# Weight loads issued in turn by SyncE and by GpSimd

## The chip, the cores and the metric

The kernel runs on one core of a Trainium2 chip. The metric is the device time of one execution in microseconds. The kernel before took 2195.15 us as the median of three runs (2191.74, 2195.15 and 2196.63 us).

## The reference, cut to what matters

The program is a decoder trunk of two layers on 256 tokens of width 2048, all in float32:

```python
# layer 0
proj  = h @ even_w_in                       # 2048 -> 4096: pool | q | k | v
mixed = concat(pool_mixer(p), stick_breaking_attention(q, k, v))
h = layer_norm(a * h + mixed @ even_w_out)
h = layer_norm(a * h + (silu(h @ w_gate) * (h @ w_up)) @ w_down)      # 5632 wide
# layer 1
z = gelu(h @ odd_w_in); u, v = split(z)
h = layer_norm(a * h + (u * (W_s @ layer_norm(v) + b)) @ odd_w_out)
for e in range(8):                          # every expert, 1408 wide, top 2 of 8 per token
    y += gates[:, e] * swiglu(h, w_gu[e], w_down[e])
h = layer_norm(a * h + y)
```

Some 520 MB of weights are read once each, and nearly all work is the products with them.

## The kernel before, in words

A weight matrix is cut into pieces of 128 rows by up to 4 x 512 columns (1 MB; some of 768 KB in the experts, and small ones at the start). The helper `load` (line 99) handles one piece: it takes a buffer `raw` (a pool of 5, line 894), starts the DMA into it (line 108), lets ScalarE round it to the high part `wh` (line 109), and subtracts to get the low part `wl` (line 117). `wh` and `wl` have 4 buffers each (line 895). The subtraction is VectorE's; a few, named by `plan` around the layer norms, and the second half of the last, shorter piece of each expert's down projection (`tail`) are GpSimd's. `raw` becomes free when the subtraction has read it, and the DMA that next takes that buffer waits for that.

For every slice of 128 rows TensorE runs three products (`mm3`, lines 126 to 128): x high by `wh`, x high by `wl`, x low by `wh`. A 1 MB piece is 12 matmuls of 512 columns for each tile of 128 tokens. In the dense stages each piece serves two token tiles, so 24 matmuls. In the experts the tokens of an expert are gathered by a matmul with a selection matrix into one tile of 128, so a piece serves 12 matmuls only. Expert by expert there are 24 pieces for gate and up and 12 for down (four blocks of three: 1 MB, 1 MB, 768 KB), 288 pieces in all, after 231 pieces before them.

The stages follow each other in one stream: the input projection with attention and pooling beside it, the output projection, the feed-forward part, the gating layer with its two projections, the routing, eight experts, the final norm. The order of instructions on each engine is made by a list scheduler when the program is built, from its own estimates; an engine works through its list in order and waits at the head of it. All DMAs are SyncE's: weight pieces, the inputs at the start (`xraw`, line 287), the norms' rows (`gb`, line 179), and the output (line 746). GpSimd's list holds 38 subtractions, some work of the routing and of the final norm, and nothing else.

At the end of the program stands a branch for experts with more than 128 tokens; it is not entered with these inputs.

Of the kernel before, what the change touches and what calls it, by code (L numbers as in the profile page):

```python
# [74 lines left out]
class Trunk:  # L75
# [23 lines left out]
    def load(self, src, w=CB, tail=None):  # L99

        nc = self.nc
        fence, planned = self.plan.pop(0) if self.plan else (None, nc.vector)
        src = src.rearrange("p (k n) -> p k n", n=w)
        kc = src.shape[1]
        raw = self.praw.tile([P, kc, w], F32, tag="raw", name="raw")
        wh = self.pw.tile([P, kc, w], F32R, tag="wh", name="wh")
        wl = self.pw.tile([P, kc, w], F32R, tag="wl", name="wl")
        nc.sync.dma_start(raw, src)
        nc.scalar.copy(wh, raw)  # L109
        if tail is not None:  # L110
            cuts = [(0, tail, nc.vector), (tail, kc, nc.gpsimd)]
        elif planned is nc.gpsimd:
            cuts = [(k, min(k + HALF, kc), planned) for k in range(0, kc, HALF)]
        else:
            cuts = [(0, kc, planned)]
        for a, b, eng in cuts:
            self.after(eng.tensor_tensor(wl[:, a:b, :], raw[:, a:b, :], wh[:, a:b, :].bitcast(F32), ALU.subtract),  # L117
                       fence)
        return wh, wl, kc
# [768 lines left out]
    def build(self):  # L888
        nc, ctx, i = self.nc, self.ctx, self.i
        e = ctx.enter_context  # L890
        pc = e(self.pool("const"))
        self.psm = e(self.pool("small"))
        self.pln = e(self.pool("ln", 2))
        self.praw = e(self.pool("raw", 5))
        self.pw = e(self.pool("w", 4))
        self.punit = e(self.pool("units", 17))
        self.pacc = e(self.pool("acc", 4, space=bass.MemoryType.PSUM))
        self.pps = e(self.pool("ps", 4, space=bass.MemoryType.PSUM))
        self.c = pc.tile([P, C_MAIN], F32, tag="c", name="c")
        self.plan = []  # L900
        self.fill = []
        self.lncols = pc.tile([P, 4, KC], F32, tag="lncols", name="lncols")
        self.ident = self.c[:, C_IDENT:C_IDENT + P]
        self.iota1 = self.c[:, C_IOTA1:C_IOTA1 + P]
        nc.scalar.preload_act_table_set("natural_log_exp_and_others")
        zeros = self.unit("zeros", BF16, [P, CB])
        nc.vector.memset(zeros, 0.0)
        self.keep_busy(10, zeros)

        mlhs = self.even_mixer()  # L910
        ph = e(self.pool("h", side="right"))
        self.h = [ph.tile([P, D], F32, tag=f"h{t}", name=f"h{t}") for t in range(NT)]
        for t in range(NT):
            nc.sync.dma_start(self.h[t], i["x"][t * P:(t + 1) * P, :])
        xT, yT = {}, {}
        _, G, B = self.out_proj(i["even_w_out"], mlhs, i["even_ln1_g"], i["even_ln1_b"],
                                norm=lambda t, stats: self.ln_to_lhs(t, stats, 0, xT))
        G, B = self.ffn(xT, G, B, lambda t, stats: self.ln_to_lhs(t, stats, 1, yT))
        mlhs = self.sgu(yT, G, B)
        pm = e(self.pool("moe", side="right"))  # L920
        self.pm = pm
        self.router_prep(pm)
        stats, G, B = self.out_proj(i["odd_w_out"], mlhs, i["odd_ln1_g"], i["odd_ln1_b"], self.router_step)
        self.moe(pm, stats, G, B)
# [81 lines left out]
```

## Time and profile before

| what | value |
|---|---|
| median of 3 runs | 2195.15 us |
| the profiled execution's own time | 2192.12 us |
| its span, first to last instruction | 2190.4 us |
| TensorE busy | 2147.6 us (98%) |
| VectorE, ScalarE, GpSimd busy | 1469.1, 1143.4, 96.4 us |
| moved by DMA | 537.81 MB, all weights on one queue |
| granted TensorE clock, mean | 0.991 |

Rows of groups give line, engine, operation, tiles and count, then busy time and the mean of one in ns, then how long the engine was idle before them and who ended that. Rows of waits give who waited for whom, the total in us, how often, and the longest. The busy time of matmuls is the union of overlapping records, so the pace of TensorE is read as stretch divided by count.

### The profile page before, as it was taken

Reading aid. Unit: us, or ns where it says so; the run is one execution under the profiler, and the core shown is the slowest. Engines: PE = TensorE matmul, PEld = TensorE weight load, DVE = VectorE, ACT = ScalarE, POOL = GpSimd, SP = SyncE. Lnnn points to the kernel's source line nnn. Section 1 sums busy time; section 2 is a strip of 40 time slices with the busy share of each in tenths; the row PEclk is TensorE's granted clock in tenths of the full one; section 3 lists DMA queues with packets and bytes.
Section 4 is the critical chain, followed back from the end, with each engine's and each line's share of the span. In section 5 each row is a group of like instructions: output and inputs, shape, how many; then the busy total and the mean of one; then the engine's idle time right before and its main releaser. Section 6 shows DMA issues by size and latency. Waiting matters only on the chain.

```text
span 2190.4 us, 24556 instructions
## 1 busy us (share of the span) xinstructions
PE 2147.6 (98%) x9956; PEld 1783.0 (81%) x9956; DVE 1469.1 (67%) x1216; ACT 1143.4 (52%) x954; POOL 96.4 (4%) x56
## 2 busy tenths in 40 slices
PE   9999999999999999999999998999999999999995
PEld 7888878888888888888788886888888888888884
DVE  5444476554454654456776458888889888878988
ACT  5445355343333433343643335766766767676673
POOL 0000010000000000000100002010100100010102
PEclk9999999999999999999999999999999999999998
DMA  9544645555454554455554543899989999998995
GB/s 354 207 154 151 234 154 204 219 192 190 156 218 166 211 192 180 186 191 193 211 192 174 212 164 108 324 351 350 334 333 361 345 337 342 349 344 323 368 356 191
DMA packets 82199, 537.81 MB, mean 246 GB/s; under 512 B 9504, under 2 KB 10656, under 8 KB 28192
## 3 DMA queue, kind: packets, MB, share of 16 engines
q1 hardware_dynamic: 82080, 536.18, 65.8%
q8 instruction: 80, 1.31, 0.2%
q14 instruction: 39, 0.32, 0.0%
HBM read 534.04 MB, written 2.10 MB: 245 GB/s over the span
## 4 chain that ended last, share of the span: by engine, by line
PE 94%; DVE 5%; issue 0%; ACT 0%; DMA 0%; SPq 0%; POOL 0%; DVEq 0%; ACTq 0%; POOLq 0%
PE acc L127 29%; PE acc L128 29%; PE acc L126 29%; PE ps L168 2%; PE ps L813 1%; DVE wl L117 1%; PE ps L872 1%; PE ps L873 1%; DVE xl L162 0%; DVE stats L223 0%; DVE h L221 0%; PE ps L560 0%; PE ps L433 0%; DVE h L212 0%; DVE o L744 0%
## 5 line engine op out<-in xcount | busy, mean ns | idle before, releaser
L117 DVE TENSOR_TENSOR wl<-raw,wh 128x2048 fp32r<-128x2048 f32 (+1 forms) x516 | 1113.5, 2176 | 395.2 <-ACT wh L109 392.8
L109 ACT CAST wh<-raw 128x2048 fp32r<-128x2048 f32 (+2 forms) x519 | 935.7, 1824 | 446.4 <-PE acc L128 408.7
L127 PE MATMUL acc<-wl,xh 128*128 128x512 f32 x960 | 376.6, 392 | 5.4 <-DVE wl L117 5.4
L128 PE MATMUL acc<-wh,xl 128*128 128x512 f32 x960 | 374.8, 390 | 0.9 <-DVE xl L162 0.9
L126 PE MATMUL acc<-wh,xh 128*128 128x512 f32 x960 | 374.6, 390 | 0.5 <-ACT wh L109 0.5
L127 PE MATMUL acc<-wl,xe 128*128 128x512 f32 (+1 forms) x768 | 286.5, 373 | 0.1
L128 PE MATMUL acc<-wh,xe 128*128 128x512 f32 (+1 forms) x768 | 285.5, 372 | 0.0
L126 PE MATMUL acc<-wh,xe 128*128 128x512 f32 (+1 forms) x768 | 284.5, 371 | 0.0
L127 PE MATMUL acc<-wl,hTh 128*128 128x512 f32 x704 | 278.2, 395 | 0.8 <-DVE wl L117 0.8
L128 PE MATMUL acc<-wh,hTl 128*128 128x512 f32 x704 | 277.8, 395 | 0.0
L126 PE MATMUL acc<-wh,hTh 128*128 128x512 f32 x704 | 275.9, 392 | 0.0
L127 PEld LDWEIGHTS acc<-wl,xh 128*128 128x128 f32 x960 | 180.7, 188 | 43.1 <-DVE wl L117 6.1
L128 PEld LDWEIGHTS acc<-wh,xl 128*128 128x128 f32 x960 | 180.8, 188 | 38.2 <-DVE xl L162 1.3
L126 PEld LDWEIGHTS acc<-wh,xh 128*128 128x128 f32 x960 | 180.5, 188 | 38.6 <-ACT wh L109 1.0
L127 PEld LDWEIGHTS acc<-wl,xe 128*128 128x128 f32 x768 | 144.2, 188 | 21.9 <-DVE wl L117 1.8
L126 PEld LDWEIGHTS acc<-wh,xe 128*128 128x128 f32 x768 | 144.2, 188 | 20.5
L128 PEld LDWEIGHTS acc<-wh,xe 128*128 128x128 f32 x768 | 144.2, 188 | 19.7
L117 POOL TENSOR_TENSOR wl<-raw,wh 128x512 fp32r<-128x512 f32 (+1 forms) x38 | 75.9, 2002 | 1875.2 <-ACT wh L109 1803.6
L127 PEld LDWEIGHTS acc<-wl,hTh 128*128 128x128 f32 x704 | 132.3, 188 | 31.5 <-DVE wl L117 2.8
L126 PEld LDWEIGHTS acc<-wh,hTh 128*128 128x128 f32 x704 | 132.4, 188 | 29.2
L128 PEld LDWEIGHTS acc<-wh,hTl 128*128 128x128 f32 x704 | 132.5, 188 | 27.4
L161 ACT CAST hTh<-ps 128x512 fp32r<-128x512 f32 (+1 forms) x46 | 26.2, 569 | 182.9 <-PE ps L168 182.9
(194 smaller groups left out, 1878.7 us busy)
## 6 DMA issues: line engine op xcount, KB each, us to landing
raw<-in_odd_moe_gu_dram SPq DMA_DIRECT2D x128, 1024.0 KB, 6.6
raw<-in_even_ffn_gu_dram SPq DMA_DIRECT2D x88, 1024.0 KB, 4.8
raw<-in_odd_moe_down_dram SPq DMA_DIRECT2D x64, 1024.0 KB, 7.1
raw<-in_odd_moe_gu_dram SPq DMA_DIRECT2D x64, 768.0 KB, 6.0
raw<-in_even_ffn_down_dram SPq DMA_DIRECT2D x44, 1024.0 KB, 4.8
raw<-in_odd_w_in_dram SPq DMA_DIRECT2D x32, 1024.0 KB, 4.8
raw<-in_even_w_in_dram SPq DMA_DIRECT2D x30, 1024.0 KB, 5.4
raw<-in_odd_moe_down_dram SPq DMA_DIRECT2D x32, 768.0 KB, 6.5
```

The lines of the kernel that those rows point to most:

```text
L109: nc.scalar.copy(wh, raw)
L117: self.after(eng.tensor_tensor(wl[:, a:b, :], raw[:, a:b, :], wh[:, a:b, :].bitcast(F32), ALU.subtract), fence)
L126: mm(acc, xh, wh, start=first, stop=False)
L127: mm(acc, xh, wl, start=False, stop=False)
L128: mm(acc, xl, wh, start=False, stop=last)
L161: self.nc.scalar.copy(hi, src)
L168: self.nc.tensor.transpose(ps[:, j * P:(j + 1) * P], src[:, j * P:(j + 1) * P], self.ident)
L813: mm(o, xtok[t, c // 8][part][:, cs], Dt[t].rearrange("p a b -> p (a b)"), start=j == 0 and t == 0, stop=t == 1, skip_group_check=True)
L872: nc.tensor.matmul(ps, DT[:, t, :], yh, start=True, stop=False)
L873: nc.tensor.matmul(ps, DT[:, t, :], yl, start=False, stop=True)
```

## The change

A counter `nload` is kept, and each piece of weights is fetched by a DMA that SyncE issues when the count is odd and GpSimd when it is even. All other DMAs stay with SyncE. The size of the pieces, the buffers and the arithmetic are the same. 260 pieces stay with SyncE and 259 go to GpSimd; in the experts the even pieces, 144 of 288, are GpSimd's.

```diff
-        nc.sync.dma_start(raw, src)
+        self.nload += 1
+        (nc.sync if self.nload % 2 else nc.gpsimd).dma_start(raw, src)
...
         self.plan = []
+        self.nload = 0
```

Lines below the edit are one or two higher in the changed program (line 117 is 118, line 620 is 621). The scheduler makes a new order. From the second projection to the gate of the gating layer it is the same on TensorE, VectorE and ScalarE; in the first 60 us and in the experts it differs in places by one piece.

At the routing and in the first expert, GpSimd's list before, where `wl` is a subtraction, `xtl` and `h` are routing work (the 32 subtractions at the end are those of all experts):

```order
L540 AFFINE_SELECT sguw<-sguw 128x1024
L628 MEMSET gg 128x256
L117 TENSOR_TENSOR wl<-raw,wh 128x1024 x2
L620 TENSOR_TENSOR xtl<-h_1534,xth 128x512 x4
L645 TENSOR_TENSOR h_1535<-h_1535,gb 128x512
L646 TENSOR_TENSOR h_1535<-h_1535,gb 128x512
L620 TENSOR_TENSOR xtl<-h_1535,xth 128x512
L117 TENSOR_TENSOR wl<-raw,wh 128x512 x32
```

The same place of GpSimd's list now, up to the first of the four down blocks of the first expert:

```order
L118 TENSOR_TENSOR wl<-raw,wh 128x1024 x2
L621 TENSOR_TENSOR xtl<-h_1534,xth 128x512 x2
L109 DMA raw<-in_odd_moe_gu_dram 128x2048
L621 TENSOR_TENSOR xtl<-h_1534,xth 128x512 x2
L646 TENSOR_TENSOR h_1535<-h_1535,gb 128x512
L647 TENSOR_TENSOR h_1535<-h_1535,gb 128x512
L621 TENSOR_TENSOR xtl<-h_1535,xth 128x512
L109 DMA raw<-in_odd_moe_gu_dram 128x2048 x4
L109 DMA raw<-in_odd_moe_gu_dram 128x1536 x4
L109 DMA raw<-in_odd_moe_down_dram 128x2048
L109 DMA raw<-in_odd_moe_down_dram 128x1536
L109 DMA raw<-in_odd_moe_down_dram 128x2048
```

DMA issues now stand between the routing's subtractions, and in each down projection the four tail subtractions stand between DMA issues.

At the end of SyncE's list before, the last expert's down pieces, then the four rows of the final norm, then the output:

```order
L108 DMA raw<-in_odd_moe_down_dram 128x1536
L108 DMA raw<-in_odd_moe_down_dram 128x2048 x2
L108 DMA raw<-in_odd_moe_down_dram 128x1536
L179 DMA gb<-in_odd_ln_g_dram 128x1024 x2
L179 DMA gb<-in_odd_ln_b_dram 128x1024 x2
L746 DMA out_dram<-o 128x512 x8
```

And the end of SyncE's list now:

```order
L109 DMA raw<-in_odd_moe_down_dram 128x2048 x2
L180 DMA gb<-in_odd_ln_g_dram 128x1024
L180 DMA gb<-in_odd_ln_b_dram 128x1024
L109 DMA raw<-in_odd_moe_down_dram 128x1536
L180 DMA gb<-in_odd_ln_b_dram 128x1024
L109 DMA raw<-in_odd_moe_down_dram 128x2048 x2
L109 DMA raw<-in_odd_moe_down_dram 128x1536
L747 DMA out_dram<-o 128x512 x8
```

Three of the four rows of the final norm now stand between the last weight pieces; the fourth has gone to the seventh expert.

## Rows read from the trace of the kernel before

**Rows 1.** The page, busy time of each engine over the whole span.
```profile
PE 2147.6 (98%) x9956; PEld 1783.0 (81%) x9956; DVE 1469.1 (67%) x1216; ACT 1143.4 (52%) x954; POOL 96.4 (4%) x56
```

**Rows 2.** Stages: stretch, length, busy (count) of PE, PEld, DVE, ACT, POOL; clock, DMA share, GB/s.
```profile
0.00:55.00 55.00, 51.35 (x209) 39.94 (x210) 31.05 (x29) 30.42 (x32) 0.21 (x4) 0.97 0.91 355
...
350.00:1040.00 690.00, 690.00 (x3073) 567.93 (x3072) 375.58 (x268) 261.35 (x166) 0.00 (x0) 1.00 0.51 189
...
1420.00:2120.00 700.00, 699.47 (x3331) 592.10 (x3330) 596.07 (x391) 495.62 (x375) 53.07 (x28) 1.00 0.93 345
2120.00:2190.40 70.40, 47.39 (x218) 39.02 (x216) 58.94 (x72) 33.21 (x28) 15.24 (x9) 0.85 0.60 231
```

**Rows 3.** The page, the chain that ended last, shares of the span by engine.
```profile
PE 94%; DVE 5%; issue 0%; ACT 0%; DMA 0%; SPq 0%; POOL 0%; DVEq 0%; ACTq 0%; POOLq 0%
```

**Rows 4.** Groups by line: the casts and subtractions of all weight pieces.
```profile
L117 DVE TENSOR_TENSOR wl<-raw,wh 128x2048 fp32r<-128x2048 f32 (+1 forms) x516 | 1113.5, 2176 | 395.2 <-ACT wh L109 392.8 <-DMA gb<-in_even_ln_b_dram 1.1
L109 ACT CAST wh<-raw 128x2048 fp32r<-128x2048 f32 (+2 forms) x519 | 935.7, 1824 | 446.4 <-PE acc L128 408.7 <-issue 11.8 <-DMA raw<-in_even_w_in_dram 9.1
...
L117 POOL TENSOR_TENSOR wl<-raw,wh 128x512 fp32r<-128x512 f32 (+1 forms) x38 | 75.9, 2002 | 1875.2 <-ACT wh L109 1803.6 <-PE acc L127 71.5
```

**Rows 5.** Line 108, the weight DMAs, in the dense stretch 400 to 1000 us.
```profile
DMA to landing us min/median/max: 4.6/4.8/6.1
```

**Rows 6.** Line 108 in the experts, 1420 to 2120 us: issue duration in ns, and landing.
```profile
L108 SPq DMA_DIRECT2D raw<-in_odd_moe_gu_dram x168: 327/328/328, 1447.6 to 2117.0; - x168
L108 SPq DMA_DIRECT2D raw<-in_odd_moe_down_dram x82: 327/328/328, 1421.7 to 2051.5; - x82
...
DMA to landing us min/median/max: 4.0/6.7/8.7
```

**Rows 7.** Waits in the experts, 1420 to 2120 us.
```profile
ACT wh L109 <- PE acc L128: 41.9, 54, 1.4
...
ACT wh L109 <- DMA raw<-in_odd_moe_down_dram: 6.7, 12, 1.0
ACT wh L109 <- DMA raw<-in_odd_moe_gu_dram: 4.0, 8, 1.1
...
PEld acc L127 <- DVE wl L117: 3.0, 9, 0.5
```

**Rows 8.** Two stretches of 10 us in the experts, columns as in rows 2.
```profile
1430.00:1440.00 10.00, 10.00 (x46) 7.95 (x46) 9.84 (x8) 7.03 (x7) 3.46 (x2) 1.00 1.00 417
...
1600.00:1610.00 10.00, 10.00 (x46) 8.28 (x45) 6.71 (x4) 6.48 (x5) 0.00 (x0) 1.00 0.71 250
```

**Rows 9.** Timeline of the start: SyncE's first and third weight issue, TensorE's matmul on the third piece.
```profile
0.82 0.39 SPq L108 DMA_DIRECT2D raw<-in_even_w_in_dram  x1
...
2.67 0.43 SPq L108 DMA_DIRECT2D raw<-in_even_w_in_dram  x1
...
9.53 0.80 PE L126 MATMUL acc<-wh,x0h 128*128 128x512 f32 x1 [2.38 <-ACT wh L109]
```

**Rows 10.** Waits over the whole span: GpSimd's first affine_select.
```profile
POOL sguw L540 <- issue: 6.3, 1, 6.3
```

**Rows 11.** Timeline of GpSimd at the routing.
```profile
1338.18 4.80 POOL L117 TENSOR_TENSOR wl<-raw,wh 128x1024 fp32r<-128x1024 f32 x2 [91.99 <-ACT wh L109]
...
1349.45 1.27 POOL L620 TENSOR_TENSOR xtl<-h,xth 128x512 fp32r<-128x512 f32 x1 [3.12 <-ACT xth L619]
```

**Rows 12.** Timeline of VectorE at the routing, two operations on 128x8.
```profile
1338.31 2.34 DVE L649 SCALAR_TENSOR_TENSOR lrow<-rrows,nmr 128x8 f32<-128x8 f32 x1
...
1343.45 0.21 DVE L651 SCALAR_TENSOR_TENSOR logits<-acc,lny,lrow 128x8 f32<-128x8 f32 x1
```

**Rows 13.** The page, DMA queues: packets, MB, share of 16 engines' span.
```profile
q1 hardware_dynamic: 82080, 536.18, 65.8%
```

**Rows 14.** The page, DMA issues: rows of the second layer's norms, KB and us to landing.
```profile
gb<-in_odd_ln_g_dram SPq DMA_DIRECT2D x4, 512.0 KB, 5.8
gb<-in_odd_ln_b_dram SPq DMA_DIRECT2D x4, 512.0 KB, 6.7
```

## The prediction, made before the result was known

> **What bounds the kernel now.** I read the busy times first, then the stages, the chain, the waits, and last single places in the timeline. TensorE is busy for 2147.6 of 2190.4 us [rows 1], and the chain that ended last runs through it for 94% of the span [rows 3]. The stages show how evenly: from 350 to 1040 us it never pauses, and from 1420 to 2120 us, in the experts, it pauses for 0.53 us in 700 [rows 2]. Its pace is 690 us / 3073 = 0.2245 us for a matmul, so a 1 MB piece that serves 12 matmuls lasts 2.70 us in the experts, and one that serves 24 lasts 5.4 us in the dense stages. The pauses are elsewhere: 3.65 us in the first 55 us, some 23 us at the end, the rest around the norms. So a change of the loads can win hardly anything; the question is what it can lose.
>
> The loads are far ahead in the dense stages (DMA share 0.51, 189 GB/s) and close in the experts (0.93, 345 GB/s) [rows 2]. There the five `raw` buffers turn once in 5 x 2.70 = 13.5 us. A turn needs 6.7 us from issue to landing [rows 6], 1.82 us of cast and 2.18 us of subtraction [rows 4], together 10.7 us: 2.8 us of slack. ScalarE waits for TensorE to give back a `wh` buffer 54 times (41.9 us) and for a DMA 20 times (6.7 + 4.0 = 10.7 us), and of this only 3.0 us reach TensorE's weight loads, as waits on `wl` [rows 7]. The transfer rate isn't at a ceiling: 10 us in the catch-up ran at 417 GB/s, while others ran at 250 [rows 8]. The 344 to 390 GB/s that TensorE asks for (1.05 MB / 2.70 us = 388 in the gate and up blocks, less in down and gather) are below that.
>
> **The change, part by part.** What is removed: 259 issues from SyncE at 0.33 us each [rows 6], 85 us of an engine that has nothing else to do. It is worth nothing, since the wait of a DMA is for its `raw` buffer and not for SyncE.
>
> What is added: the same 259 issues on GpSimd, which the trace of before never shows. From below, an issue costs what SyncE's does, 0.33 us. From above, it costs as much as GpSimd's own instruction on such data, 2.0 us, and waits out one VectorE subtraction of 2.18 us ahead of it [rows 4]: 4.2 us. I take 1.0 us, nearer to the issue than to the subtraction, since an issue doesn't touch the data. GpSimd has room: 96.4 + 259 x 1.0 = 355 us of 2190 (at 4.2 us 1184 us).
>
> The Trainium skill, "DMA: Bandwidth & Descriptors", section "Issuing engines are not separate DMA queues", says that DMAs of all issuers run on the same 16 engines and that several issuers save the issuing time only; and its specifications give the first byte at about 1 us for GpSimd and 0.6 us for SyncE. By these figures the addition would be 0.4 us per moved load, within the bounds above, and no rate would be won. No run here shows it yet.
>
> Dense stages, 55 to 1340 us: a turn of five buffers lasts 5 x 5.4 = 27 us and needs 4.8 [rows 5] + 1.82 + 2.18 = 8.8 us. 18 us of slack cover 0.67 or 3.9 us more. Cost 0. Without that cover, each late piece would stop TensorE.
>
> Experts: a `raw` buffer is filled by SyncE and GpSimd in turn, so 1.0 - 0.33 = 0.67 us falls on every second turn, 0.34 us in the mean against 2.8 us of slack; at the upper bound (4.2 - 0.33 = 3.9) it is 1.9 us in the mean, still inside. What is left are the 20 places where a cast waits for its DMA already: half of them are GpSimd's, 10 x 0.67 = 6.7 us. Of such waits 3.0 / 10.7 reach TensorE now, so 1.9 us; I take 2. Bounds: 0, and 10 x 3.9 = 39 us if all reach it.
>
> GpSimd's own list: a tail subtraction (2.0 us) now stands ahead of a DMA and a DMA ahead of a tail. In the down blocks the DMA that follows a tail needs the buffer of a piece whose subtraction ends about when the tail starts, so it is late by 2 us or less, eight DMAs or fewer per pair of experts and each inside the 2.8 us. At the routing the DMA that stands between two `xtl` falls into a gap of 3.12 us in which GpSimd waited for ScalarE [rows 11]: 1.0 us fits, 4.2 us would come out 1.1 us late, on the path to the gather. I take 0 for both.
>
> Start: the third piece arrives last of the first three, and TensorE waits 2.38 us for it [rows 9]. SyncE now issues it about 0.45 us earlier, with one issue less ahead, but the fourth piece (512 KB) is then in flight beside it and takes up to 0.52 MB / 355 GB/s = 1.5 us of its rate. From -0.5 to +1.5 us: I take +0.5. GpSimd's first issue may be slow: its first affine_select came after 6.3 us in which nothing held it [rows 10]. If the second piece had that ahead of it, TensorE would start some 4.5 us later. That is the upper bound, and -2.4 us, the whole wait, the lower.
>
> End: three rows of the final norm now go out between the last weight pieces, 3 x 0.52 MB, which at 345 GB/s is 4.6 us of transfer that was behind them (they took 5.8 and 6.7 us to land [rows 14]). In the last 70 us VectorE is the busy one (58.9 us [rows 2]), with little slack. I take 1.5 us, between 0 and 4.6.
>
> Sum: 0.5 + 2 + 0 + 1.5 = 4.0 us on the profiled execution's 2192.12 us (span 2190.4 and 1.7 around it), so 2196.1. That execution lies 3.0 us under the median of the runs shown, 2195.15; from the median the forecast is 2199 us. A measurement of this kernel can tell some 0.2%, 4.4 us, from no change: the forecast is "no change", leaning to slower. Its own range is 2192 to 2203.
>
> **Rivals.** A, slower: an issue on GpSimd stops VectorE. For it speaks that GpSimd's subtraction does: the small operation on 128x8 elements took 2.34 us beside it, and 0.21 us without it [rows 11, 12]. If each issue held VectorE for 1.0 us, the 125 issues of the 700 us (half of 168 + 82 [rows 6]) would add 125 us where VectorE has 700 - 596 = 104 us idle [rows 2]. If all the idle time can be used the stage grows by 21 us, if half of it by 73; in the middle 47 us, 2242 us. It decides only in the experts; elsewhere VectorE is busy to 55%. Against it: an issue reads no tile. The Trainium skill, "SBUF — State Buffer", section "Who interferes with whom", says that a VectorE instruction with two SBUF inputs contends with a GpSimd instruction that reads SBUF, not with one that only writes; the 2.34 us agree with its first half, and by its second this rival falls, which no row here shows.
>
> B, slower: two queues lose the order. Before, one queue holds all [rows 13], and the piece needed first lands first. With two, the engines serve both, and of a pair in flight both land at the end: the first is later by one transfer, 1.05 MB / 417 GB/s = 2.5 us, 1.25 us in the mean of a pair. With the 0.34 us that is still under the 2.8 us of slack; with the upper 1.9 us it is 3.2 us, over it by 0.4. 288 / 5 = 58 turns at 0.4 us are 23 us: 2218 us. The point from which it decides is a median landing above 6.7 + 2.8 = 9.5 us in the experts. For it speaks that slack is thin there, against it that landing already varies from 4.0 to 8.7 us [rows 6] and TensorE loses 0.53 us.
>
> C, faster: the new order and the second issuer bring the first pieces earlier and nothing else is late. At most 2.4 us at the start and 3.0 us of waits on `wl` in the experts are to be had, 2190 us; only both together pass the 4.4 us.
>
> **How the numbers follow.** The forecast has 0.55, A 0.12, B 0.23, C 0.10. Of the forecast's own cases about a tenth end above the 4.4 us, since its sum stands at 4.0 already: 0.49 stay within, 0.06 go to slower. Of C 0.08 count as faster and 0.02 as no change. So faster 0.08, same 0.51, slower 0.41. For 8 in 10 the range reaches from C's 2190 to 2228, past B and short of A's middle; the upper bounds of the experts (39 us) and of the start (4.5 us) lie partly outside.
>
> **What would show it.** Right: a second queue in the table with half of the weight bytes; TensorE still without pauses from 350 to 1040 us and within 3 us of it in the experts; landing in the experts under 9.5 us; the end longer by 1 or 2 us. A shows as VectorE instructions that grow beside issues and a subtraction mean above 2.3 us. B shows as casts that wait for DMAs for far more than 10.7 us. A long wait of the second or third matmul group in the first 12 us shows a slow first issue. The forecast is wrong if the experts' 700 us grow by more than 6 us, or if TensorE's pace leaves 0.2245 us.

## The result and the profile after

The changed kernel takes 2214.23 us (median of 4 runs, 2211.73 to 2216.78) against 2195.70 us for the kernel before beside it (4 runs, 2191.74 to 2196.63): a ratio of 1.0087, 95% interval [1.0072, 1.0102], so 18.5 us more. The forecast was 2199 with a range from 2190 to 2228; the likeliest case, no change, didn't come, and "slower" had 0.41. The profiled execution took 2213.55 us with a span of 2211.9.

First the page, its busy times and its queues, against [rows 1, 13]:

```profile
PE 2151.2 (97%) x9956; PEld 1781.3 (81%) x9956; DVE 1472.3 (67%) x1216; ACT 1154.8 (52%) x954; POOL 240.6 (11%) x315
...
q1 hardware_dynamic: 44784, 278.47, 34.0%
q0 software_dynamic: 37232, 257.70, 31.7%
```

The change does what it says: nearly half of the bytes are in a second queue. No engine has become the bound; GpSimd has 144 us more to do in 2212. The stages tell where the time is, with the columns of [rows 2]:

```profile
0.00:55.00 55.00, 48.38 (x186) 36.71 (x187) 27.04 (x27) 26.92 (x29) 4.65 (x12) 0.91 0.84 329
350.00:1040.00 690.00, 690.00 (x3073) 568.00 (x3072) 373.10 (x265) 261.29 (x166) 32.94 (x62) 1.00 0.53 191
1420.00:2120.00 700.00, 687.03 (x3263) 578.58 (x3262) 589.92 (x386) 498.51 (x370) 123.48 (x151) 1.00 0.91 341
2120.00:2211.90 91.90, 66.53 (x308) 54.82 (x306) 72.12 (x80) 44.88 (x36) 21.32 (x18) 0.90 0.59 227
```

The dense stretch is untouched: TensorE without a pause, to the same number of matmuls. The start has 186 matmuls in 55 us instead of 209. In the experts TensorE now pauses for 13 us in 700, where it paused for 0.5. The bytes per second there are no more than before (341 against 345 GB/s). By the Trainium skill, "DMA: Bandwidth & Descriptors", "Issuing engines are not separate DMA queues", several issuers save issuing time and win no rate; this trace agrees.

Between the first and the last gather lie nearly six of the eight experts, without the start and the end, which makes a good ruler. The gathers' matmuls on xth (the high part of the tokens), of the kernel before and then of the changed one (duration in ns: shortest, median, longest; then first and last start in us):

```profile
L813 PE MATMUL ps<-Dt,xth x128: 276/280/372, 1359.4 to 1964.7; 128*128 128x256 f32 x128
```
```profile
L814 PE MATMUL ps<-Dt,xth x128: 277/280/387, 1363.3 to 1982.4; 128*128 128x256 f32 x128
```

So 3.9 us are lost before the first gather, 13.8 between the two (619.1 against 605.3), and 3.8 behind the last (229.5 against 225.7 to the end of the span). The two profiled runs lie 21.5 us apart, the medians 18.5.

The chain that ended last is no longer TensorE's alone [rows 3]. These are its engines, and two of the transfers that it names in the experts (start, duration):

```profile
PE 87%; DVE 5%; DMA 4%; ACT 2%; issue 1%; SPq 0%; POOL 0%; ACTq 0%; DVEq 0%; POOLq 0%
```
```profile
1731.47 10.05 DMA raw<-in_odd_moe_down_dram
1839.02 10.33 DMA raw<-in_odd_moe_down_dram
```

There are nine such rows, all of down weights, one per expert and a second one of 11.91 us at the end. The waits, from 1425 to 2175 us (total, times, longest), say the same, against [rows 7]:

```profile
ACT wh L110 <- DMA raw<-in_odd_moe_down_dram: 29.1, 31, 3.4
...
PEld ps L169 <- DVE silu L514: 11.0, 9, 1.9
...
PE ps L169 <- DVE silu L514: 7.4, 6, 1.5
...
PE ps L814 <- ACT xe L816: 3.7, 3, 2.8
...
ACT wh L110 <- DMA raw<-in_odd_moe_gu_dram: 3.2, 3, 1.2
```

Casts wait 29 us for down weights instead of 7, those of gate and up wait no longer than they did. But TensorE doesn't stop at a weight load for it: it waits for the silu product and for gathered tokens. One such place, on ScalarE in the changed kernel (start, duration, what, and in brackets the idle time before it; silu is the activation of a block of the gate, hTh the high part of the block's transposed product, which is TensorE's operand for the down projection):

```profile
1839.19 0.48 ACT L513 ACTIVATE silu<-acc 128x384 f32<-128x384 f32 x1
1839.88 1.92 ACT L110 CAST wh<-raw 128x2048 fp32r<-128x2048 f32 x1 [0.21 <-PE acc L129]
1843.45 1.92 ACT L110 CAST wh<-raw 128x2048 fp32r<-128x2048 f32 x1 [1.65 <-DMA raw<-in_odd_moe_down_dram]
1846.48 1.47 ACT L110 CAST wh<-raw 128x1536 fp32r<-128x1536 f32 x1 [1.12 <-DMA raw<-in_odd_moe_down_dram]
1849.46 1.91 ACT L110 CAST wh<-raw 128x2048 fp32r<-128x2048 f32 x1 [1.50 <-DMA raw<-in_odd_moe_down_dram]
1851.27 0.47 ACT L162 CAST hTh<-ps 128x384 fp32r<-128x384 f32 x1
```

and the same place in the kernel before:

```profile
1825.53 0.49 ACT L512 ACTIVATE silu<-acc 128x384 f32<-128x384 f32 x1 [2.21 <-PE acc L128]
1825.92 2.85 ACT L109 CAST wh<-raw 128x1536 fp32r<-128x1536 f32 x2
1829.52 1.92 ACT L109 CAST wh<-raw 128x2048 fp32r<-128x2048 f32 x1 [0.75 <-DMA raw<-in_odd_moe_down_dram]
1832.02 1.92 ACT L109 CAST wh<-raw 128x2048 fp32r<-128x2048 f32 x1 [0.58 <-DMA raw<-in_odd_moe_down_dram]
1835.15 0.48 ACT L161 CAST hTh<-ps 128x384 fp32r<-128x384 f32 x1 [1.21 <-PE ps L168]
```

Two things differ. The transfers come later, and the list has another order: hTh, which TensorE needs next, stood behind two casts of down weights and waited for TensorE; now it stands behind four and waits, through them, for transfers. On VectorE the silu product moved in the same way. In the order of the lists silu, hTh, their products and remainders stand one or two pieces later in every expert but the first; "in places by one piece", as said ahead of the prediction, was too little. The scheduler that writes the lists did this by itself when half of the loads changed queue.

The transfer in the chain, the fourth piece of the down weights, can be looked at by itself. While it was in flight, 1839.02 to 1849.36 us, the engines moved (packets, MB, share):

```profile
DMA packets 628, 4.21 MB, mean 407 GB/s; under 512 B 63, under 2 KB 63, under 8 KB 270
...
q1 hardware_dynamic: 345, 2.39, 56.7%
q0 software_dynamic: 281, 1.80, 41.8%
```

and for the same piece before, 1829.21 to 1836.80 us:

```profile
DMA packets 476, 3.21 MB, mean 423 GB/s; under 512 B 52, under 2 KB 52, under 8 KB 185
...
q1 hardware_dynamic: 474, 3.18, 100.5%
```

The rate is nearly the same. But 1.0 MB more of other pieces went by before this one was complete: 1.0 MB / 407 GB/s = 2.5 us of the 10.33 - 7.59 = 2.7 us. At an equal rate a longer flight always has more bytes beside it; what this shows is that the engines were no slower, so the time went to other pieces. Over the first four down pieces of experts 1 to 6 the median from issue to landing on SyncE's queue is 8.5 us (12 pieces), on GpSimd's 7.4 (12), and 7.0 before (24). These compare different places, since GpSimd's are the first and the third of the four. Place by place the medians were 6.1, 6.9, 7.2 and 7.4 us before and are 7.1, 8.3, 8.3 and 9.2 now: SyncE's own pieces, which weren't moved, come 1.4 and 1.8 us later, GpSimd's 1.0 and 1.1.

### The profile page after: what moved, and what is told of

It is laid out like the page before. It is cut to its first block, busy times and chain, and to the rows that moved or that the text cites. A ratio compares the mean times of both kernels' runs of the same rounds, so it can differ in the third digit from the quotient of the medians.

```text
span 2211.9 us, 24599 instructions
## 1 busy us (share of the span) xinstructions
PE 2151.2 (97%) x9956; PEld 1781.3 (81%) x9956; DVE 1472.3 (67%) x1216; ACT 1154.8 (52%) x954; POOL 240.6 (11%) x315
## 4 chain that ended last, share of the span: by engine, by line
PE 87%; DVE 5%; DMA 4%; ACT 2%; issue 1%; SPq 0%; POOL 0%; ACTq 0%; DVEq 0%; POOLq 0%
PE acc L128 27%; PE acc L129 27%; PE acc L127 27%; DMA raw<-in_odd_moe_down_dram 4%; DVE wl L118 2%; PE ps L169 1%; ACT wh L110 1%; PE ps L814 1%; PE ps L874 1%; PE ps L873 1%; DMA xraw<-in_xT_dram 0%; DVE xl L163 0%; PE ps L561 0%; PE ps L434 0%; DVE h L213 0%
## 5 line engine op out<-in xcount | busy, mean ns | idle before, releaser
L118 DVE TENSOR_TENSOR wl<-raw,wh 128x2048 fp32r<-128x2048 f32 (+1 forms) x516 | 1116.6, 2166 | 423.8 <-ACT wh L110 420.8
L110 ACT CAST wh<-raw 128x2048 fp32r<-128x2048 f32 (+2 forms) x519 | 946.1, 1824 | 583.3 <-PE acc L129 524.7
L127 PEld LDWEIGHTS acc<-wh,hTh 128*128 128x128 f32 x704 | 132.4, 188 | 29.1
L127 PE MATMUL acc<-wh,x0h 128*128 128x512 f32 x256 | 105.4, 412 | 5.0 <-ACT wh L110 4.1
L118 POOL TENSOR_TENSOR wl<-raw,wh 128x512 fp32r<-128x512 f32 (+1 forms) x38 | 81.9, 2157 | 184.9 <-ACT wh L110 183.1
```

The costliest lines, as they stand in the source:

```text
L127: mm(acc, xh, wh, start=first, stop=False)
```

## The experiments

Theory O: the order of the lists. Theory S (Q in the first two expectations): two queues share the engines, so the piece needed first lands later. Theory L: transfers stand behind tail subtractions in GpSimd's list. Theory P: GpSimd's queue is slower by itself. Ratios are to the kernel before on the same chip, with 95% intervals; the last column is the ruler, first to last gather, of one profiled run.

| kernel | median us | ratio | ruler us |
|---|---|---|---|
| before | 2193.2 to 2195.7 | 1 | 605.3 |
| changed | 2214.23 | 1.0087 [1.0072, 1.0102] | 619.1 |
| e1 two queues, old order | 2210.13 | 1.0076 [1.0062, 1.0089] | 613.6 |
| e2 one queue, new order | 2200.30 | 1.0029 [1.0020, 1.0038] | 610.9 |
| e3 start on SyncE | 2210.36 | 1.0073 [1.0060, 1.0086] | 619.4 |
| e4 two queues ahead of the experts | 2199.93 | 1.0022 [1.0013, 1.0031] | 606.9 |
| e5 experts all GpSimd's | 2213.33 | 1.0079 [1.0065, 1.0093] | 619.3 |
| e6 two queues for gate and up | 2199.35 | 1.0017 [1.0008, 1.0025] | 609.8 |
| e7 e1, tails on VectorE | 2213.98 | 1.0085 [1.0072, 1.0098] | 612.7 |
| e8 before, tails on VectorE | 2194.41 | 0.9996 [0.9987, 1.0005] | 607.0 |
| e9 experts all GpSimd's, tails on VectorE | 2199.79 | 1.0027 [1.0015, 1.0038] | 609.9 |
| e10 two queues for down | 2201.89 | 1.0042 [1.0030, 1.0054] | 607.8 |
| e11 two queues, loads 9 to 231 | 2197.16 | 1.0014 [1.0005, 1.0023] | 607.7 |
| e12 each piece on both queues | 2405.06 | 1.0950 [1.0929, 1.0971] | 760.5 |

The ruler has scatter of its own: e4 and e11 have one queue and the old order in the experts, as the kernel before, and stand at 606.9 and 607.7 against its 605.3. Differences of 2 or 3 us on it say nothing.

**Order against queues.** e1 forces the old places of the experts' casts and subtractions: the cast or subtraction of piece p + 1 may not stand ahead of the operation that had piece p ahead of it before. e2 forces the new places on the kernel with one queue.

```diff
+            todo += [(self.casts, silu[b], m[0]), (self.subs, mul[b], m[1]),
+                     (self.casts, hth[b], m[2]), (self.subs, htl[b], m[3])]
...
+            for seq, p, ins in todo:
...
+                    self.after(seq[base + p], ins)        # e1; e2: self.after(ins, seq[base + p - 1])
```

> Two queues as in the changed kernel, but in the experts the casts, subtractions and each block's own operations (silu, its product, hTh, hTl, yh, yl, the sums into h) stand on ScalarE and VectorE in the order of the kernel before; start and end as in the changed kernel. Theory O (the order of the two lists is the cause: an operation that TensorE needs stands behind casts and subtractions of later pieces, which wait for a transfer): first to last gather returns from 619 us to about 605, and the time falls by some 14 us to 2200 us (start and end keep 4 us each). Theory Q (the two queues are the cause: the piece needed first lands later, whatever the order): the casts still wait some 25 us for pieces of the down weights, first to last gather stays at 619 us, and the time stays at 2214 us.

> One queue, SyncE's, as in the kernel before, but in the experts the casts and subtractions of later pieces stand ahead of each block's own operations, as in the changed kernel; start and end as in the kernel before. Theory O: first to last gather grows from 605 us to about 619 and the time to 2209 us. Theory Q: 605 us and 2195 us, within 2 us. If both share the cause, between: some 2200 us.

Neither theory holds alone. The order costs 0.29% with one queue, 6.4 us; giving the old order back to two queues wins 0.11% (1.0087 to 1.0076), 2.4 us, less than the intervals can tell. By the ruler it is 5.6 and 5.5 us. Both edits did what they should. Counted in the traces, the 80 operations silu, hTh and yh of the eight experts stand on ScalarE behind the same number of casts in e1 as in the kernel before, and in e2, but for one, as in the changed kernel. The idle time ahead of silu, when ScalarE stands ready and waits for TensorE, is there in e1 as in the kernel before (47.9 us), and gone in e2 as in the changed one (0.0). The lines are ScalarE's silu in e1 and in e2 (count, busy, mean ns, idle before):

```profile
L517 ACT ACTIVATE silu<-acc 128x512 f32<-128x512 f32 (+1 forms) x22 | 12.3, 559 | 52.8 <-PE acc L132 52.8
```
```profile
L517 ACT ACTIVATE silu<-acc 128x512 f32<-128x512 f32 (+1 forms) x22 | 12.2, 554 | 0.0
```

**Start and dense stages.** e3 and e4 change one condition, `self.nload < 9` or `self.nload > 231` on SyncE.

```diff
-        (nc.sync if self.nload % 2 else nc.gpsimd).dma_start(raw, src)
+        (nc.sync if self.nload % 2 or self.nload < 9 else nc.gpsimd).dma_start(raw, src)     # e3
+        (nc.sync if self.nload % 2 or self.nload > 231 else nc.gpsimd).dma_start(raw, src)   # e4
```

> As the changed kernel, but the first eight loads are all SyncE's. If the start's 4 to 5 us come from the second to fourth pieces standing in two queues beside the activations, the first real matmul group's waits are those of the kernel before and the time is 2209 to 2210 us, with the experts at 619 us still. If they come from anything else of the start (GpSimd's later issues, the granted clock by itself), 2214 us.

> Two queues for the 231 loads ahead of the experts, SyncE alone from there. Both theories of the experts: first to last gather 605 us. The dense stages with two queues cost nothing beside the start, so 2195.5 + 4 to 5 = 2200 us; 2195 us would say that the start's loss is taken in later, and over 2203 us that the dense stages lose too.

Both came as expected. The start is worth 0.14% (from 1.0087 to 1.0073) to 0.22% (e4), 3 to 5 us; the 0.14% alone is within the intervals, but the traces bear it out. The first gather starts at 1363.0 to 1364.0 us in the four profiled runs with two queues at the start (changed, e1, e4, e7) and at 1358.7 to 1361.8 us in the ten others, 3.1 us apart in the mean. The scheduler wrote the experts' lists of e4 in the old order, so the new order isn't a matter of the dense loads. In the start of the changed kernel the first issues, and the casts and matmuls that wait, are:

```profile
0.94 0.39 SPq L109 DMA_DIRECT2D raw<-in_even_w_in_dram  x1
...
1.48 1.26 POOL L109 DMA_DIRECT2D raw<-in_even_w_in_dram  x2 [0.83 <-POOLq L994]
2.32 0.43 SPq L109 DMA_DIRECT2D raw<-in_even_w_in_dram  x1
...
7.44 0.62 ACT L110 CAST wh<-raw 128x512 fp32r<-128x512 f32 x1 [3.06 <-DMA raw<-in_even_w_in_dram]
8.11 0.50 PE L127 MATMUL acc<-wh,x0h 128*128 128x512 f32 x1 [1.41 <-ACT wh L110]
...
11.12 1.04 ACT L110 CAST wh<-raw 128x1024 fp32r<-128x1024 f32 x1 [2.44 <-DMA raw<-in_even_w_in_dram]
12.22 0.79 PE L127 MATMUL acc<-wh,x0h 128*128 128x512 f32 x1 [2.65 <-ACT wh L110]
```

GpSimd issues the second and the fourth piece by 2.7 us, ahead of SyncE's third and most of the activations. The second piece lands at 7.42 us instead of 4.92, the third at 11.10 instead of 8.41; in the other three runs with two queues at the start the second lands at 6.0 to 6.5 us, in those with one at 4.5 to 5.8. This fits theory S at another place: more is in flight, and what is needed next shares with what isn't.

TensorE's clock has a part in it. These are the first 20 us of the kernel before and of the changed one:

```profile
0.00:20.00 20.00, 16.36 (x56) 11.24 (x57) 9.82 (x16) 11.88 (x19) 0.21 (x4) 0.91 0.88 317
```
```profile
0.00:20.00 20.00, 13.38 (x32) 7.72 (x33) 8.98 (x16) 9.66 (x17) 3.05 (x9) 0.74 0.87 319
```

In both the granted clock fell to its lower level, 1.2 GHz, at 9.1 and 9.5 us, behind the first waits for casts. Before, it rose again at 12.5 us; in the changed kernel only at 19.7 us, with waits of 2.65 and 0.95 us in between. There matmuls start 0.43 us apart instead of 0.23, 12 times instead of 5, so an estimate of the clock's part is 7 x 0.2 = 1.4 us, and the rest of the start's loss are the waits themselves. The mean clock of these 20 us varies between the profiled runs, from 0.83 to 1.00 with one queue at the start and from 0.74 to 0.91 with two.

**GpSimd's list or its queue.** e5 gives all 288 loads of the experts to GpSimd, in the old order; e7 is e1 with the tails on VectorE, e8 its base with one queue, and e9 is e5 with the tails on VectorE.

```diff
+        (nc.sync if self.nload < 232 else nc.gpsimd).dma_start(raw, src)     # e5, e9
...
-            cuts = [(0, tail, nc.vector), (tail, kc, nc.gpsimd)]
+            cuts = [(0, kc, nc.vector)]                                      # e7, e8, e9
```

> SyncE's queue alone for the 231 loads ahead of the experts, GpSimd's queue alone for all 288 of the experts; the lists of ScalarE and VectorE in the experts in the order of the kernel before. It tells apart what is left of the experts' loss in the old order with two queues (first to last gather 613.6 us against 605.3). Theory S (sharing: a piece shares the 16 DMA engines with the next piece of the other queue and lands later): with one queue that is gone, 606 us, and 2197 us in all. Theory L (GpSimd's list: transfers stand behind the tail subtractions of 1.6 to 2.3 us there): twice as many stand behind them, so 614 to 622 us and 2205 to 2213 us.

> Two queues with the old order in the experts, but the tail subtractions are VectorE's, so GpSimd's list holds nothing but transfers in the experts. VectorE gets 28 x 0.6 us more in 700 us, where it is idle for some 75 us. Against the same with one queue (e8_tails_on_vector_one_queue). Theory L: both have the same first to last gather within 2 us, and this one is 4 to 6 us longer in all, for the start. Theory S: this one is still 7 to 9 us longer between the gathers and 13 to 16 us in all.

> The kernel before (SyncE's queue alone, the order of before in the experts) with the tail subtractions on VectorE instead of GpSimd: the base of e7_tails_on_vector. Both theories: 2195 to 2200 us, since VectorE has room for 17 us in the experts; first to last gather 605 to 609 us.

> SyncE's queue for the 231 loads ahead of the experts, GpSimd's queue alone for the 288 of the experts, the old order, and the tail subtractions on VectorE (base: e8_tails_on_vector_one_queue, 2194.4 us, 607.0 us from first to last gather). GpSimd's list holds nothing but transfers, and one queue holds all of the experts. Theory S (pieces of two queues share the engines): no loss, 606 to 609 us and 2194 to 2198 us. Theory P (GpSimd's queue itself is slower, by its issue or otherwise): the loss of e5 stays, 613 to 619 us and 2203 to 2213 us.

e5 is as slow as the changed kernel with no sharing at all, at the upper end of what L expected. GpSimd's rows in e5 show why: after a tail three transfers go out back to back, whose buffers had come free while it stood ahead of them.

```profile
1642.27 2.34 POOL L119 TENSOR_TENSOR wl<-raw,wh 128x512 fp32r<-128x512 f32 x1 [5.26 <-ACT wh L110]
1644.56 1.62 POOL L109 DMA_DIRECT2D raw<-in_odd_moe_down_dram  x3
1650.66 2.34 POOL L119 TENSOR_TENSOR wl<-raw,wh 128x512 fp32r<-128x512 f32 x1 [4.48 <-ACT wh L110]
1652.95 1.62 POOL L109 DMA_DIRECT2D raw<-in_odd_moe_down_dram  x3
```

With the tails gone (e9) 0.52% of this is gone, 11 us. But with two queues the tails don't matter: e7 (1.0085) is no faster than e1 (1.0076), and its base e8 is no slower than before. So L is true of a kernel that gives GpSimd all, and not the cause in this change; there the one transfer in two that is GpSimd's is seldom the one behind a tail. Worked out from the issue times in experts 1 to 6, 72 of 216 transfers in e5 went out more than 0.6 us after their buffer came free, 12 of 108 in e1 and 14 of 108 in the changed kernel. Tails on VectorE were tried in the old order alone. The ruler of e7 is 5.7 us over that of e8 and its time 19.6 us: L expected less than 2 and 4 to 6, S 7 to 9 and 13 to 16, so the time is above both.

e9 lies between S and P: 0.31% over its base e8, 6.8 us, less than P expected, and with one queue and no tails it is P's. Worked out from the issue times, GpSimd issues 0.41 us after the subtraction that frees the buffer (median), SyncE 0.03, and the first four down pieces land in 7.6 us (24 pieces) against 7.2 in e8. The waits for down weights, of e9 and then of e8:

```profile
ACT wh L110 <- DMA raw<-in_odd_moe_down_dram: 19.2, 22, 2.0
```
```profile
ACT wh L110 <- DMA raw<-in_odd_moe_down_dram: 10.6, 12, 2.6
```

Two queues without tails (e7 over e8) cost 0.89%, of which 0.22% are the start (e4), so 0.67% or 14.7 us in the experts and at the end. If P costs half of e9's 6.8 us where GpSimd has half of the pieces, some 11 us are left for S, by this difference; that half is assumed and not measured. S shows more directly in SyncE's own pieces. The second of the four down pieces is SyncE's before as with two queues, and its median from issue to landing in experts 1 to 6 is 6.9 us before and 7.0 in e8, but 8.7 in e1, 8.6 in e7 and 8.0 in e10.

**Which pieces.** e6 and e10 have two queues in the experts alone, for gate and up or for down, in the old order, and SyncE's in the dense stages.

```diff
+        (nc.sync if self.nload % 2 or self.nload < 232 or (self.nload - 232) % 36 > 23 else nc.gpsimd).dma_start(raw, src)  # e6
+        (nc.sync if self.nload % 2 or self.nload < 232 or (self.nload - 232) % 36 < 24 else nc.gpsimd).dma_start(raw, src)  # e10
```

> Two queues as in the changed kernel with the old order in the experts, but all 96 pieces of the down weights are SyncE's; gate and up pieces alternate. Theory S: the late pieces are those of the down weights, which now follow each other in one queue, but the next expert's gate and up pieces still share with them: 607 to 610 us from first to last gather, 2203 to 2206 us. Theory L: hardly any transfer of GpSimd's stands behind a tail, 606 us and 2200 us. If the loss stands in the gate and up pieces, 614 us and 2210 us.

> SyncE's queue for everything but every second piece of the down weights, which is GpSimd's; the old order; tails on GpSimd as before. Theory S: sharing decides where the slack is used up, at the first pieces of the down weights, so most of e1's loss in the experts is here: 610 to 613 us from first to last gather, 2201 to 2206 us. If the gate and up pieces carried it, 605 to 607 us and 2195 to 2198 us.

The expectation of e6 reckoned with the start of the changed kernel, which e6 doesn't have; without those 4 us S expected 2199 to 2202, and it is 2199.35. A third of the pieces, the down weights, cost 0.42%, and the other two thirds 0.17%: 9.2 and 3.7 us, together 12.9, against 11.9 for e1 less e4. e10's total is as S expected, its ruler is not: 607.8 us, with most of its loss behind the last gather in the profiled run (231.2 us to the end of the span, where before has 225.7). That run took 2199.93 us, near the fastest of six (2198.81 to 2206.32).

**Where there is slack, and both queues on one piece.**

```diff
+        (nc.sync if self.nload % 2 or not 8 < self.nload < 232 else nc.gpsimd).dma_start(raw, src)      # e11
...
+        for eng, a, b in ((nc.sync, 0, P // 2), (nc.gpsimd, P // 2, P)) if self.nload > 231 else ((nc.sync, 0, P),):
+            eng.dma_start(raw[a:b], src[a:b])                                                           # e12
```

> Two queues for loads 9 to 231 alone: neither the start nor the experts. Theory S: pieces land later there too, but 18 us of slack cover it, so nothing is lost: 2195 us within 3 us, 605 us from first to last gather. A remaining loss over 4 us would say that a second queue costs something that has nothing to do with slack.

> In the experts each piece is two transfers of 64 partitions, one on SyncE's queue and one on GpSimd's, so both queues work on the same piece; the old order, tails on VectorE, SyncE alone ahead of the experts (base: e8_tails_on_vector_one_queue). Theory S: the pieces keep their order although there are two queues, so nothing is lost, 605 to 609 us from first to last gather and 2194 to 2198 us. If two queues or GpSimd's issues cost by themselves: 612 us and more, 2203 us and more.

e11 is 0.14% slower, 3.1 us, with an interval from 1.1 to 5.0: inside the 4 us that were set, with the upper end of the interval beyond them. Its profiled run takes 2195.26 us and shows no loss where the second queue is: the first gather starts at 1358.7 us, before at 1359.4. Whether the second queue costs a little where there is slack stays open. In e12 S expected no loss, and the loss is far beyond the other case too (612 us and more). So it tells nothing of S, because it brought a larger effect of its own; whether half the partitions, half the size or the two queues make it isn't told apart. A half of 64 partitions (512 KB) takes 13 us to land where a whole piece took 7 with the tails on VectorE. From 1425 to 2125 us, with the columns of [rows 2]:

```profile
1425.00:2125.00 700.00, 599.45 (x2654) 476.62 (x2655) 480.58 (x316) 403.04 (x308) 101.14 (x198) 0.97 1.02 273
```

The engines are busy all the time and move 273 GB/s, where [rows 2] has 345 at a share of 0.93.

No kernel of these is faster than the kernel before; e8 is equal to it.

## Why the prediction was right and wrong

**The loads win nothing, and the question is what they lose**: right. Removing 85 us of SyncE's issues was worth nothing that a run shows.

**An issue on GpSimd, 1.0 us**: it is 0.53 us, within the bounds of 0.33 and 4.2. From the freed buffer to the landing a moved piece takes about 0.8 us more (e9 against e8): 0.41 us instead of 0.03 until the issue starts, and some 0.4 us more from there. That is near the 0.67 forecast.

**Dense stages, 0**: right as far as the traces show (690.00 us of 690, and e11's first gather no later than before), with e11's 3.1 us not placed.

**Start, +0.5**: mis-sized; 3 to 5 us, at the upper bound of 4.5, though not by the mechanism of that bound: GpSimd's first two issues took 1.26 us together. The sum had no term for the clock either. I let one piece share with the third. There were three needed in turn, and the second, which I let come as before, landed 2.5 us later.

**Experts, +2, which is the step that failed.** It held 0.67 us of delay, on the moved pieces alone, against 2.8 us of slack, and the slack was a mean over the 700 us. The delay falls on the others too (SyncE's second and fourth down pieces land 1.4 and 1.8 us later), and the slack isn't there where it counts. At the end of gate and up a 768 KB piece lasts 12 matmuls of 384 columns, so buffers come free every 2.08 us (the casts in the changed kernel stand 1834 to 1840 at that distance), and the 1 MB pieces of down are asked for at 1.05 MB / 2.08 us = 504 GB/s while 407 to 423 are moved. Already before, 12 of the 24 casts of the first four down pieces in experts 1 to 6 started within 0.2 us of the landing. Those pass a delay on. The stage lost 13.8 us by the ruler, inside the bounds of 0 and 39, and more than the 6 us that were to tell that the forecast is wrong. The measured 2214 us is also outside the forecast's own range of 2192 to 2203; the wide range holds it because that was drawn past rival B.

**The order of the lists** has no term in the sum: the prediction priced moved transfers and tails but not that silu, hTh and the product come to stand behind one or two casts or subtractions more. e2 measures 6.4 us for it alone; on top of two queues it is 2.4 us (the changed kernel against e1), which may be nothing. The three parts (start 4.8, order 6.4, queues 11.9) make 23 us, more than the 18.5 measured; that order and queues lose partly the same time, at the same place in each expert, is argued from e1 and e2 and not shown.

**GpSimd's list, 0**: right for two queues in the old order (e7 against e1), not tried in the new one, and wrong for a kernel with all loads on GpSimd (e5 against e9, 11 us).

**End, +1.5**: 3.8 us from the last gather to the end, in which two experts lie too. At the ruler's 13.8 us for six experts these two would lose 4.6 us, so nothing is left that shows a loss of the end itself. A down piece at 2154.19 us took 11.91, with rows of the final norm between the last pieces; how much of it is theirs was not tried.

**Rival A** (VectorE stopped by issues, 2242 us) fell: the mean subtraction went from 2176 ns [rows 4] to 2166, VectorE's busy time from 1469 to 1472 us. In the changed kernel the 128x2048 subtractions beside a GpSimd issue took 2292 ns (median of 86), those beside nothing of GpSimd's 2293 (317). The Trainium skill, "SBUF — State Buffer", "Who interferes with whom", has a VectorE instruction with two SBUF inputs contend with a GpSimd instruction that reads SBUF, not with one that only writes it. For an issue this trace agrees.

**Rival B** (two queues lose the order, 2218 us) names the mechanism of the larger part: pieces needed first land later, by 2.7 us in the piece looked at, where B had 2.5. That its time is so near is luck. B came to 23 us by the upper price of an issue (1.9 us in the mean), spread over 58 turns. At the 0.8 us measured its own sum would be 1.25 + 0.4 = 1.65 us against 2.8 of slack, and no loss; it failed on the same mean slack as the forecast. And the start and the order of the lists, which B hadn't, are in the 18.5 us. Its sign was wrong too: I wanted a median landing over 9.5 us in the experts, and the median stayed at 6.7 with a longest of 10.3. It decides at one place per expert, and a median over the stage doesn't see that. The other sign, casts that wait for DMAs for far more than 10.7 us, came: 29.1 + 3.2 us from 1425 to 2175 us.

## What to carry to other kernels

Take slack from the place where the demand changes, here from small pieces to large ones, and not from a stage's mean. Where several pieces are in flight and the rate doesn't rise, a second queue only decides who lands first; here one queue in the order of need was better. When a load changes its queue, look at what the scheduler does to the lists of the other engines, since an operation that stands behind a waiting cast waits too.

## What the hardware did that was not expected

- Pieces split by partitions over two queues moved slowly (e12): 273 GB/s with all DMA engines busy (share 1.02), against 345 at a share of 0.93.
- A single queue of GpSimd's cost 6.8 us more than a single one of SyncE's in the experts (e9 over e8), with 0.53 us per issue against 0.33, and an issue 0.41 us after its buffer came free against 0.03.
